# Weight-block sums by accumulating transfers in a seven-product feed-forward kernel

## The chip, the cores and the metric

The kernel runs on one core of one Trainium2 chip. A core has a matrix engine (TensorE; PE in the profile, its weight loads PEld), VectorE (DVE), ScalarE (ACT), GpSimd (POOL) and SyncE (SP), which here only issues transfers. Sixteen DMA engines move data between DRAM and the on-chip memory (SBUF); transfers can be issued from the queues of SP, ACT and POOL. The metric is the device time of one execution in microseconds (us); lower is better.

## The reference

One step of a two-layer decoder trunk over 544 tokens (512 of a prompt, 32 of samples), model width 1024. Each layer is a half feed-forward, a mixer and another half feed-forward, so there are four feed-forward phases, all of this form:

```python
def swiglu(x, w_gu, w_down):
    gate, up = jnp.split(x @ w_gu, 2, axis=-1)
    return (jax.nn.silu(gate) * up) @ w_down

def macaron_half(h, g, w_gu, w_down):
    return h + 0.5 * swiglu(rms_norm(h, g), w_gu, w_down)
```

`w_gu` is 1024 x 5632 (2816 gate columns, then 2816 up columns), `w_down` 2816 x 1024, all in float32. The mixer of the first layer is a gated MLP beside a state-space scan; that of the second is pooling beside windowed attention, whose scores get a bias from a small table by distance. In the kernel that bias is a skewed view of a pattern of 16 heads x 383 values, written 128 times in a row to DRAM.

## The kernel before, in words

**Products.** Every operand is split into a rounded part `h` and a remainder `l`; a product is three matmuls per 128 rows of the contraction (h·h, h·l, l·h). The splits of weights are `wparts` (ACT makes `wh` at L234, DVE makes `wl` at L235).

**Seven products for eight.** The gate and up matmul is done by a Strassen-like scheme. A block `f` is 128 gate and 128 up columns (22 blocks a phase, 88 in all). Its weights form a 2 x 2 of blocks: gate or up, by even or odd 128-row tiles of the contraction (`g0, g1, u0, u1`). The other operand is a 2 x 2 too: even or odd tiles, by the two halves of the tokens (272 each). Four of the seven left operands are sums of weight blocks, made on GpSimd (`sums7`, L224 to L227): S1 = u0 + u1, S2 = S1 - g0, S3 = g0 - u0, S4 = g1 - S2. The right operands' sums are made on DVE by `pair7` (L325 to L328). Each product runs over 4 tiles, 12 matmuls.

**Staging.** `load7` brings a block with two transfers of 512 KB on SP's queue into a stage tile `S` (two buffers); the sums lie in pool `sp` (one buffer each before). The split weights lie in pool `wu` (12 buffers each of `wh` and `wl`). The last operand of a block read from `S` is A22, so it frees the stage for the block two further on. The pools `wu`, `sd`, `sp`, `hl` and `rot` of a feed-forward group share memory with the pools of the mixer before it; the stage does not.

**Order.** `ffn` runs a list of jobs: per block seven products in the order A11, S2, S3, S1, A12, S4, A22 (A22 after the first job of the next block), and between them the down products of the parts that are ready. Loads are traced 17 jobs ahead of the matmuls (`LOADS`), splits 10 (`AHEAD`). The first block of a phase makes six products together (`p_first`). A planner turns the traced program into one fixed order per engine, by priorities and a simulated timeline; on the chip each engine follows its order and waits where data isn't there yet. Copies out of PSUM and gate functions are traced with high priority on ACT and DVE, among the splits.

**Groups.** The phases run as f10, even mixer, f20 and f11 (one group, so f11's loads run ahead of the border), odd mixer, f21.

**Side work.** During f10, from job 12 on, `ffn` advances a generator `mid` by one step per job. It loads four rows of parameters from ACT's queue (L408), later transposes them, and then makes the bias pattern (`bias_pattern`): small loads on POOL, one matmul, one add (L1161), and one transfer of 3064 KB from 16 partitions of SBUF to DRAM on POOL's queue (L1163). At the beginning GpSimd also adds up the squares for the norm (L307, L309).

Of the kernel before, what the change touches and what calls it, by code (L numbers as in the profile page):

```python
# [92 lines left out]
class Trunk:  # L93
    MIX = lambda r, a, u, l: (("wp", "wp", 2), ("rot", "rot", r), ("aux", "aux", a), ("uu", "uu", u), ("ld", "ld", l),
                              ("sm", "sm", 1))
    POOLS = {"even": MIX(4, 18, 3, 5), "odd": MIX(6, 14, 4, 5)}
    POOLS["f"] = (("wu", "wu", 12), ("sd", "sd", 2), ("sp", "sp", 1), ("hl", "hl", 7), ("rot", "rot", 7))

    RIGHT = {"A11": "B11", "S2": "T2", "S3": "T3", "S1": "T1", "A12": "B21", "S4": "B22", "A22": "N4"}
    PARTS = ((0, 3), (3, 6), (6, 9), (9, 12), (12, 15), (15, 18), (18, 22))  # L100
# [110 lines left out]
    def load7(self, w, f):  # L211

        s = self.stg.tile([P, 8, 256], F32, name=self.nm("S"), tag="S")
        for q in range(2):
            c0 = q * DFF + f * P
            self.nc.sync.dma_start(s[:, :, q * P:(q + 1) * P], w[:, c0:c0 + P].rearrange("(k p) m -> p k m", p=P))
        return s

    def sums7(self, s):

        G = self.nc.gpsimd
        g0, g1, u0, u1 = s[:, 0::2, 0:P], s[:, 1::2, 0:P], s[:, 0::2, P:], s[:, 1::2, P:]
        t = {n: self.sp.tile([P, 4, P], F32, name=self.nm(n), tag=n) for n in ("S1", "S2", "S3", "S4")}
        G.tensor_tensor(t["S1"], u0, u1, op=ALU.add)  # L224
        G.tensor_tensor(t["S2"], t["S1"], g0, op=ALU.subtract)  # L225
        G.tensor_tensor(t["S3"], g0, u0, op=ALU.subtract)  # L226
        G.tensor_tensor(t["S4"], g1, t["S2"], op=ALU.subtract)  # L227
        return {"A11": g0, "A12": g1, "A22": u1, **t}

# [52 lines left out]

    def gain(self, n, k):
        c = self.col[("ffn1_norm", "mix_norm", "ffn2_norm")[n % 3]]
        return c[:, n // 3 * 8 + k:n // 3 * 8 + k + 1]
# [28 lines left out]
    def pair7(self, j, n):  # L314

        nc = self.nc
        S, V, G = nc.scalar, nc.vector, nc.gpsimd
        x0, x1 = self.x[2 * j], self.x[2 * j + 1]
        g0, g1 = self.gain(n, 2 * j), self.gain(n, 2 * j + 1)
        A, B, D, E = (self.tmp(s) for s in ("fa", "fb", "fd", "fe"))  # L320
        lo_, hi_ = slice(0, HT), slice(HT, T)
        S.activation(A[:, lo_], x0[:, lo_], AF.Copy, scale=g0)
        S.activation(E[:, lo_], x0[:, hi_], AF.Copy, scale=g0)  # L323
        S.activation(B, x1, AF.Copy, scale=g1)
        V.tensor_tensor(A[:, hi_], E[:, lo_], A[:, lo_], op=ALU.subtract)  # L325
        V.tensor_tensor(D[:, lo_], B[:, hi_], A[:, hi_], op=ALU.subtract)
        V.tensor_tensor(D[:, hi_], B[:, hi_], E[:, lo_], op=ALU.subtract)
# [5 lines left out]
        for src, names in ((A, ("B11", "T1")), (B, ("B21", "B22")), (D, ("T2", "T3"))):  # L333
# [105 lines left out]
    def pair_jobs(self, gu, f, first, ph):  # L439
# [72 lines left out]
        def p_first():  # L512
# [89 lines left out]
    def ffn(self, steps, mid=None):  # L602
# [4 lines left out]
        for i, (_, _, run) in enumerate(jobs):  # L607
# [540 lines left out]
    def bias_pattern(self):  # L1148
# [13 lines left out]
        scr = self.dr.tile([16, P * 383], F32, name="scr")  # L1162
        nc.gpsimd.dma_start(scr.rearrange("h (r e) -> h r e", e=383), self.bc(pat[:16, :383], 1, P))  # L1163
        self.skew = scr[:, 127:127 + P * 382].rearrange("h (r e) -> h r e", e=382)
# [490 lines left out]
```

## Time and profile before

| | before |
|---|---|
| median of 3 runs | 2374.7 us (2369.0 to 2376.09) |
| the profiled execution | 2374.62 us, its span 2372.8 us |
| mean granted TensorE clock | 0.972 |
| busy: PE, DVE, ACT, POOL | 2267.3, 1802.6, 1099.4, 683.8 us |
| moved by DMA | 224.23 MB, mean 94 GB/s |
| GpSimd adds of weight blocks (L224 to L227) | 352, between 118.4 and 142.5 us per line |
| the bias pattern's transfer | 3064 KB, 33.5 us from issue to landing |

The span runs from the first to the last instruction of the profiled execution. In the rows of the profile a group is a line of the kernel with its engine, operation, written and read tiles, the count after an x, busy time, mean duration in ns, and after the bar the idle time before it with what ended it. A queue (SPq, POOLq) is an engine's issuing side. The share of DMA is the mean busy share of the 16 engines.

### The profile page before, as it was taken

The numbers are of one execution on the slowest core, as the hardware profiler recorded it, in microseconds if no ns is written. First come the engines' busy times: TensorE is split into PE (matmuls) and PEld (weight loads), VectorE is DVE, ScalarE is ACT, GpSimd is POOL, SyncE is SP. The second block draws the span as 40 slices with busy tenths as digits, with TensorE's granted clock in tenths as the row PEclk, the third lists the DMA queues.
The fourth block names the chain that finished last, engine by engine and source line by source line (L and its number), as shares of the span: only waits on it lengthen the run. The fifth ranks groups of instructions, "written<-read, shape, count | busy, mean of one in ns | idle before, by whom it ended". The sixth has DMA issues, their size and how long they took to land.

```text
span 2372.8 us, 43129 instructions
## 1 busy us (share of the span) xinstructions
PE 2267.3 (96%) x17292; PEld 2183.8 (92%) x17292; DVE 1802.6 (76%) x2993; ACT 1099.4 (46%) x2106; POOL 683.8 (29%) x551
## 2 busy tenths in 40 slices
PE   4969999999999989999998999999999998999998
PEld 3969999998779989999998999999988988999998
DVE  8958887766457769888879988886478657988884
ACT  4524444444336454444446444444255555444442
POOL 5323331004331015333323333322033004333331
PEclk6989999999999999999999999999999988999999
DMA  3453323321432222332331323234313213232321
GB/s 106 97 110 101 105 82 102 123 75 55 124 115 91 93 85 88 102 105 88 98 110 54 105 88 98 87 101 135 121 54 102 92 58 101 82 105 87 105 83 65
DMA packets 309241, 224.23 MB, mean 94 GB/s; under 512 B 11256, under 2 KB 301392, under 8 KB 309040
## 3 DMA queue, kind: packets, MB, share of 16 engines
q1 hardware_dynamic: 302856, 203.85, 28.2%
q0 software_dynamic: 5936, 17.55, 3.0%
q8 instruction: 135, 2.21, 0.4%
q14 instruction: 66, 0.54, 0.1%
q10 hardware_dynamic: 248, 0.07, 0.0%
HBM read 203.69 MB, written 17.75 MB: 93 GB/s over the span
## 4 chain that ended last, share of the span: by engine, by line
PE 79%; DVE 8%; issue 7%; DMA 3%; ACT 1%; POOL 1%; SPq 0%; POOLq 0%; DVEq 0%; ACTq 0%
PE acc L206 39%; PE ps L244 33%; DVE wl L235 2%; DMA S<-in_ffn_w_gu_dram 2%; DVE l L254 1%; PE ps L1118 1%; PE ps L1350 1%; PE ps L1394 1%; PE ps L827 1%; PE ps L1389 1%; PE ps L819 0%; PE ps L348 0%; ACT wh L234 0%; DVE wl L192 0%; PE acc L244 0%
## 5 line engine op out<-in xcount | busy, mean ns | idle before, releaser
L244 PE MATMUL ps<-h,wh 128*128 128x272 f32 x2384 | 690.0, 291 | 35.2 <-ACT u L480 19.3
L244 PE MATMUL ps<-l,wh 128*128 128x272 f32 x2384 | 690.0, 290 | 0.0
L244 PE MATMUL ps<-h,wl 128*128 128x272 f32 x2384 | 685.1, 290 | 0.0
L206 PE MATMUL acc<-h,wh 128*128 128x272 f32 x2832 | 600.6, 293 | 9.0 <-ACT wh L191 3.4
L206 PE MATMUL acc<-l,wh 128*128 128x272 f32 x2832 | 601.7, 292 | 0.5 <-DVE l L254 0.5
L234 ACT ACTIVATE wh<-S 128x512 fp32r<-128x512 f32 x616 | 381.3, 629 | 469.6 <-PE ps L244 270.3
L206 PE MATMUL acc<-h,wl 128*128 128x272 f32 x2832 | 596.6, 291 | 0.4 <-DVE wl L192 0.4
L235 DVE TENSOR_TENSOR wl<-S,wh 128x512 fp32r<-128x512 f32 x616 | 534.3, 877 | 67.9 <-ACT wh L234 65.7
L244 PEld LDWEIGHTS ps<-h,wh 128*128 128x128 f32 x2384 | 452.8, 190 | 40.2 <-ACT u L480 19.9
L206 PEld LDWEIGHTS acc<-h,wh 128*128 128x128 f32 x2832 | 448.2, 190 | 21.9 <-issue 11.2
L206 PEld LDWEIGHTS acc<-l,wh 128*128 128x128 f32 x2832 | 449.9, 190 | 11.3 <-issue 9.6
L206 PEld LDWEIGHTS acc<-h,wl 128*128 128x128 f32 x2832 | 448.6, 189 | 6.7 <-issue 5.3
L244 PEld LDWEIGHTS ps<-l,wh 128*128 128x128 f32 x2384 | 453.6, 190 | 0.3
L244 PEld LDWEIGHTS ps<-h,wl 128*128 128x128 f32 x2384 | 451.9, 190 | 0.0
L226 POOL TENSOR_TENSOR S<-S 128x512 f32<-128x512 f32 x88 | 135.6, 1541 | 654.1 <-DMA S<-in_ffn_w_gu_dram 434.5
L557 DVE SCALAR_TENSOR_TENSOR x<-acc,x 128x544 f32<-128x544 f32 x224 | 160.4, 717 | 105.9 <-PE acc L206 105.5
L235 DVE TENSOR_TENSOR wl<-D,wh 128x384 fp32r<-128x384 f32 (+1 forms) x224 | 188.8, 846 | 39.3 <-ACT wh L234 30.5
L224 POOL TENSOR_TENSOR S<-S 128x512 f32<-128x512 f32 x88 | 142.5, 1619 | 254.1 <-ACT fe L323 118.2
L234 ACT ACTIVATE wh<-D 128x384 fp32r<-128x384 f32 (+1 forms) x224 | 119.6, 537 | 169.8 <-PE ps L244 128.8
L191 ACT ACTIVATE wh<-S 128x1024 fp32r<-128x1024 f32 x89 | 93.3, 1050 | 197.9 <-PE acc L206 156.4
L227 POOL TENSOR_TENSOR S<-S,S 128x512 f32<-128x512 f32 x88 | 118.4, 1345 | 121.4 <-DVE wl L235 120.3
L225 POOL TENSOR_TENSOR S<-S,S 128x512 f32<-128x512 f32 x88 | 126.9, 1442 | 6.6 <-DVE wl L235 0.7
(466 smaller groups left out, 2413.9 us busy)
## 6 DMA issues: line engine op xcount, KB each, us to landing
S<-in_ffn_w_gu_dram SPq DMA_DIRECT2D x176, 512.0 KB
D<-in_ffn_w_down_dram SPq DMA_DIRECT2D x96, 384.0 KB
S<-in_ev_w_in_dram SPq DMA_DIRECT2D x18, 1024.0 KB
S<-in_od_w_in_dram SPq DMA_DIRECT2D x10, 1024.0 KB
D<-in_ffn_w_down_dram SPq DMA_DIRECT2D x16, 512.0 KB
S<-in_ev_w_out_dram SPq DMA_DIRECT2D x8, 1024.0 KB
S<-in_od_w_out_dram SPq DMA_DIRECT2D x8, 1024.0 KB
xd<-x POOLq DMA_DIRECT2D x16, 272.0 KB, 2.5
```

The source lines that it names most:

```text
L191: nc.scalar.activation(hi[:, :nk, :n], src, AF.Copy)
L206: self.nc.tensor.matmul(acc[a][:, :HT] if type(acc) is list else acc[:, a, :HT], w[:, k, :], r[:, a * HT:(a + 1) * HT], start=k == order[0 ...
L224: G.tensor_tensor(t["S1"], u0, u1, op=ALU.add)
L225: G.tensor_tensor(t["S2"], t["S1"], g0, op=ALU.subtract)
L226: G.tensor_tensor(t["S3"], g0, u0, op=ALU.subtract)
L227: G.tensor_tensor(t["S4"], g1, t["S2"], op=ALU.subtract)
L234: self.nc.scalar.activation(hi, src, AF.Copy)
L235: self.nc.vector.tensor_tensor(lo, src, hi.bitcast(F32), op=ALU.subtract)
L244: self.nc.tensor.matmul(acc, a[:, j, :], r, start=start and j == 0 and q == 0, stop=stop and j == 3 and q == 2, skip_group_check=True)
L254: nc.vector.tensor_tensor(l, src, h.bitcast(F32), op=ALU.subtract)
L557: nc.vector.scalar_tensor_tensor(two(self.x[m]), acc[:, :, :HT], 0.5, two(self.x[m]), op0=ALU.mult, op1=ALU.add)
L827: PE.matmul(psy[:, hh * 64:hh * 64 + 64], es[hh // 4][:, (hh % 4) * P:(hh % 4 + 1) * P], xd[:, hh * 64:hh * 64 + 64], start=True, stop=True)
```

## The change

It has three parts.

1. `sums7` is gone. `load7` now issues six loads on SP's queue (512 KB of gate rows into the stage, 256 KB each into S1, S2, S3, S4 with one of their terms, 256 KB of u1) and then four accumulating transfers on POOL's queue: S1 += u1 and S3 += g0 from DRAM, S2 += S1 and S4 += S2 inside SBUF. S1 lies in the half of the stage that u0 used to fill. `sp` holds three tiles with two buffers each for four with one; `wu` has 11 buffers for 12.
2. An accumulate only adds, so the signs move: `pair7` scales with negated gains (two more columns made once), its differences become sums and negated sums, and the gate rows come out negative, which `Silu` undoes with `scale=-1.0`.
3. The bias pattern goes out in 16 transfers of 8 rows each, one per step of the generator. `ffn` queues what a step issues on POOL behind the latest S4 accumulate (`self.late`) traced so far; the parameter rows are loaded from POOL's queue for ACT's.

```diff
-    POOLS["f"] = (("wu", "wu", 12), ("sd", "sd", 2), ("sp", "sp", 1), ("hl", "hl", 7), ("rot", "rot", 7))
+    POOLS["f"] = (("wu", "wu", 11), ("sd", "sd", 2), ("sp", "sp", 2), ("hl", "hl", 7), ("rot", "rot", 7))
...
-        for q in range(2):
-            c0 = q * DFF + f * P
-            self.nc.sync.dma_start(s[:, :, q * P:(q + 1) * P], w[:, c0:c0 + P].rearrange("(k p) m -> p k m", p=P))
-        return s
-
-    def sums7(self, s):
-
-        G = self.nc.gpsimd
-        g0, g1, u0, u1 = s[:, 0::2, 0:P], s[:, 1::2, 0:P], s[:, 0::2, P:], s[:, 1::2, P:]
-        t = {n: self.sp.tile([P, 4, P], F32, name=self.nm(n), tag=n) for n in ("S1", "S2", "S3", "S4")}
-        G.tensor_tensor(t["S1"], u0, u1, op=ALU.add)
-        G.tensor_tensor(t["S2"], t["S1"], g0, op=ALU.subtract)
-        G.tensor_tensor(t["S3"], g0, u0, op=ALU.subtract)
-        G.tensor_tensor(t["S4"], g1, t["S2"], op=ALU.subtract)
-        return {"A11": g0, "A12": g1, "A22": u1, **t}
+        v = w.rearrange("(j q p) m -> q p j m", q=2, p=P)
+        g, u = slice(f * P, (f + 1) * P), slice(DFF + f * P, DFF + (f + 1) * P)
+        t = {n: self.sp.tile([P, 4, P], F32, name=self.nm(n), tag=n) for n in ("S2", "S3", "S4")}
+        t["S1"] = s[:, 4:8, P:]
+        nc.sync.dma_start(s[:, :, 0:P], w[:, g].rearrange("(k p) m -> p k m", p=P))
+        for n, q, c in (("S1", 0, u), ("S2", 0, g), ("S3", 0, u), ("S4", 1, g)):
+            nc.sync.dma_start(t[n], v[q, :, :, c])
+        nc.sync.dma_start(s[:, 0:4, P:], v[1, :, :, u])
+        nc.gpsimd.dma_start(t["S1"], v[1, :, :, u], accum_op=ALU.add)
+        nc.gpsimd.dma_start(t["S3"], v[0, :, :, g], accum_op=ALU.add)
+        nc.gpsimd.dma_start(t["S2"], t["S1"], accum_op=ALU.add)
+        self.late = nc.gpsimd.dma_start(t["S4"], t["S2"], accum_op=ALU.add)
+        return {"A11": s[:, 0::2, 0:P], "A12": s[:, 1::2, 0:P], "A22": s[:, 0:4, P:], **t}
...
-        V.tensor_tensor(A[:, hi_], E[:, lo_], A[:, lo_], op=ALU.subtract)
-        V.tensor_tensor(D[:, lo_], B[:, hi_], A[:, hi_], op=ALU.subtract)
-        V.tensor_tensor(D[:, hi_], B[:, hi_], E[:, lo_], op=ALU.subtract)
-        V.tensor_tensor(E[:, hi_], B[:, lo_], D[:, lo_], op=ALU.subtract)
+        V.tensor_tensor(A[:, hi_], E[:, lo_], A[:, lo_], op=ALU.add)
+        V.scalar_tensor_tensor(D[:, lo_], B[:, hi_], -1.0, A[:, hi_], op0=ALU.mult, op1=ALU.subtract)
+        V.tensor_tensor(D[:, hi_], E[:, lo_], B[:, hi_], op=ALU.add)
+        V.scalar_tensor_tensor(E[:, hi_], B[:, lo_], -1.0, D[:, lo_], op0=ALU.mult, op1=ALU.subtract)
...
-                S.activation(st["g"], st["g"], AF.Silu)
+                S.activation(st["g"], st["g"], AF.Silu, scale=-1.0)
...
-                next(mid, None)
+                with self.tc.issue_after(self.late.ins):
+                    next(mid, None)
...
-        nc.gpsimd.dma_start(scr.rearrange("h (r e) -> h r e", e=383), self.bc(pat[:16, :383], 1, P))
+        s3 = scr.rearrange("h (r e) -> h r e", e=383)
+        for r in range(0, P, 8):
+            nc.gpsimd.dma_start(s3[:, r:r + 8], self.bc(pat[:16, :383], 1, 8))
+            yield
...
-        yield from self.columns_gen(("b_norm_g", "c_scale", "a_ln_g", "a_ln_b"), self.TT)
+        yield from self.columns_gen(("b_norm_g", "c_scale", "a_ln_g", "a_ln_b"), self.TT, self.nc.gpsimd)
```

More of the change, by code (lines that the diff above doesn't have):

```diff
@@ L96 @@
     POOLS = {"even": MIX(4, 18, 3, 5), "odd": MIX(6, 14, 4, 5)}
-    POOLS["f"] = (("wu", "wu", 12), ("sd", "sd", 2), ("sp", "sp", 1), ("hl", "hl", 7), ("rot", "rot", 7))
-    RIGHT = {"A11": "B11", "S2": "T2", "S3": "T3", "S1": "T1", "A12": "B21", "S4": "B22", "A22": "N4"}
+    POOLS["f"] = (("wu", "wu", 11), ("sd", "sd", 2), ("sp", "sp", 2), ("hl", "hl", 7), ("rot", "rot", 7))
+    RIGHT = {"A11": "N11", "S2": "T2", "S3": "N3", "S1": "T1", "A12": "N21", "S4": "N22", "A22": "N4"}
     PARTS = ((0, 3), (3, 6), (6, 9), (9, 12), (12, 15), (15, 18), (18, 22))
@@ L281, in rsqrt_small, with gain @@
             self.newton(out if i == 2 else r, r, ms, t)
-    def gain(self, n, k):
-        c = self.col[("ffn1_norm", "mix_norm", "ffn2_norm")[n % 3]]
+    def gain(self, n, k, sign=""):
+        c = self.col[sign + ("ffn1_norm", "mix_norm", "ffn2_norm")[n % 3]]
         return c[:, n // 3 * 8 + k:n // 3 * 8 + k + 1]
@@ L318, in pair7 @@
         x0, x1 = self.x[2 * j], self.x[2 * j + 1]
-        g0, g1 = self.gain(n, 2 * j), self.gain(n, 2 * j + 1)
+        g0, n0, n1 = self.gain(n, 2 * j), self.gain(n, 2 * j, "-"), self.gain(n, 2 * j + 1, "-")
         A, B, D, E = (self.tmp(s) for s in ("fa", "fb", "fd", "fe"))
         lo_, hi_ = slice(0, HT), slice(HT, T)
-        S.activation(A[:, lo_], x0[:, lo_], AF.Copy, scale=g0)
+        S.activation(A[:, lo_], x0[:, lo_], AF.Copy, scale=n0)
         S.activation(E[:, lo_], x0[:, hi_], AF.Copy, scale=g0)
[L324 to L327, printed above, removed]
-        V.tensor_tensor(E[:, hi_], B[:, lo_], D[:, lo_], op=ALU.subtract)
+        S.activation(B, x1, AF.Copy, scale=n1)
+        V.tensor_tensor(A[:, hi_], E[:, lo_], A[:, lo_], op=ALU.add)
+        V.scalar_tensor_tensor(D[:, lo_], B[:, hi_], -1.0, A[:, hi_], op0=ALU.mult, op1=ALU.subtract)
+        V.tensor_tensor(D[:, hi_], E[:, lo_], B[:, hi_], op=ALU.add)
+        V.scalar_tensor_tensor(E[:, hi_], B[:, lo_], -1.0, D[:, lo_], op0=ALU.mult, op1=ALU.subtract)
         if j % 2 == 0:
@@ L332, in pair7 @@
         ops = {}
-        for src, names in ((A, ("B11", "T1")), (B, ("B21", "B22")), (D, ("T2", "T3"))):
+        for src, names in ((A, ("N11", "T1")), (B, ("N21", "N22")), (D, ("T2", "N3"))):
             h, l = self.split(src)
@@ L397, in columns, with columns_gen @@
             pass
-    def columns_gen(self, names, alloc):
+    def columns_gen(self, names, alloc, eng=None):
         nc, I = self.nc, self.I
@@ L407, in columns_gen @@
             n = src.shape[0] * src.shape[1] // P
-            nc.scalar.dma_start(rows[r:r + n, :P], src.rearrange("a (m p) -> (a m) p", p=P))
+            (eng or nc.scalar).dma_start(rows[r:r + n, :P], src.rearrange("a (m p) -> (a m) p", p=P))
             off[nme] = (r, n)
@@ L418, in columns_gen @@
             self.col[k] = cols[:, o:o + n]
+            if k in ("ffn1_norm", "ffn2_norm"):
+                self.col["-" + k] = self.const.tile([P, n], F32, name=self.nm("ncol"))
+                nc.vector.tensor_scalar(self.col["-" + k], cols[:, o:o + n], -1.0, None, op0=ALU.mult)
     def store_x(self, m):
@@ L448, in load @@
         def load():
-            st["s"] = self.load7(gu, f)
+            st["t"] = self.load7(gu, f)
         def parts(n):
             def go():
-                if "t" not in st:
-                    st["t"] = self.sums7(st["s"])
                 st[n] = self.wparts(st["t"][n])
```

3 lines of the change are left out of this document (2 added, 1 removed).

## The prediction

> **What bounds the kernel now.** I read the page's totals first, then busy time in stretches of 50 us, then the chain of waits and the idle time inside the stretches that are not full. On the page:
>
> ```profile
> span 2372.8 us, 43129 instructions
> PE 2267.3 (96%) x17292; PEld 2183.8 (92%) x17292; DVE 1802.6 (76%) x2993; ACT 1099.4 (46%) x2106; POOL 683.8 (29%) x551
> PE 79%; DVE 8%; issue 7%; DMA 3%; ACT 1%; POOL 1%; SPq 0%; POOLq 0%; DVEq 0%; ACTq 0%
> ```
>
> TensorE is idle for 2372.8 - 2267.3 = 105.5 us in all; a change that removes no matmul can win that, plus the matmuls run at a lowered clock. Busy time in stretches (stretch and length, then per engine busy us and instructions in the order PE, PEld, DVE, ACT, POOL; then granted clock, DMA share, GB/s) shows where it lies:
>
> ```profile
> 50.00:100.00 50.00, 44.21 (x312) 41.93 (x312) 47.23 (x65) 26.77 (x50) 22.27 (x17) 0.92 0.25 74
> 100.00:150.00 50.00, 31.46 (x236) 30.46 (x236) 23.25 (x39) 12.94 (x26) 9.58 (x8) 0.84 0.77 129
> 200.00:250.00 50.00, 50.00 (x402) 50.00 (x401) 39.85 (x62) 23.20 (x45) 17.67 (x14) 1.00 0.32 96
> 850.00:900.00 50.00, 42.50 (x318) 41.39 (x317) 39.61 (x57) 26.20 (x47) 12.73 (x8) 0.93 0.27 80
> 900.00:950.00 50.00, 45.83 (x339) 45.01 (x338) 45.54 (x67) 24.33 (x49) 24.78 (x16) 0.93 0.30 88
> 1250.00:1300.00 50.00, 41.97 (x278) 39.42 (x277) 46.89 (x80) 31.68 (x59) 12.10 (x8) 0.90 0.22 64
> 1950.00:2000.00 50.00, 43.60 (x314) 42.35 (x313) 34.71 (x54) 25.47 (x44) 17.85 (x11) 0.93 0.27 79
> 2000.00:2050.00 50.00, 44.79 (x331) 43.81 (x330) 47.84 (x69) 26.18 (x51) 19.69 (x14) 0.93 0.31 90
> ```
>
> The third row is the feed-forward (FFN) steady state: TensorE full, clock 1.00, 402 matmuls in 50 us, POOL at 17.67. There neither a faster VectorE nor a free GpSimd moves the end. The others are short of 402, and (402 - n) x 50/402 gives their price: 20.6 us at 100 to 150, 11.2 at 50 to 100, 18.3 at 850 to 950, 15.4 at 1250 to 1300, 19.8 at 1950 to 2050. The gains have to come from there.
>
> **The hole at 100 to 150.** The chain, the GpSimd issue and its landing, and fine stretches:
>
> ```profile
> 107.25 33.95 DMA S<-in_ffn_w_gu_dram
> 106.45 1.04 POOL L1163 DMA_DIRECT2D scr<-pat  x1 [2.40 <-DVE pat L1161]
> scr<-pat POOLq DMA_DIRECT2D x1, 3064.0 KB, 33.5
> 126.00:128.00 2.00, 2.00 (x18) 2.00 (x17) 0.00 (x0) 0.00 (x0) 0.00 (x0) 1.00 1.00 112
> 128.00:130.00 2.00, 0.68 (x6) 0.46 (x4) 0.00 (x0) 0.00 (x0) 0.00 (x0) 1.00 0.97 110
> 140.00:142.00 2.00, 0.00 (x0) 0.00 (x0) 0.00 (x0) 0.00 (x0) 0.63 (x1) 0.50 1.12 359
> PE ps L244 <- ACT u L480: 18.5, 1, 18.5
> ```
>
> The bias pattern holds all DMA engines (share 1.00, but 112 GB/s) for 33.5 us; a weight load issued a moment later lands only behind it, at 359 GB/s. TensorE lives on prepared operands until 128.7, 22 us after the issue, then idles 18.5 us and restarts at clock 0.50. Its line names ACT, which itself sits behind a late sum in its queue.
>
> **The change, part by part.** *Bias pattern in 16 parts.* Engine time stays 33.5 us, 2.1 us a part. Each part is queued on POOL behind the latest S4 accumulate traced so far, one part per job, and a block has 7 + 56/22 = 9.5 jobs. So some 9 parts, 19 us, may leave back to back after one block's S4 and the rest a block later. 19 us is less than the 22 us TensorE lasted, so most of the hole closes; accumulates behind a burst in the same queue are late, which keeps part of it. Ends: 0 (parts still make one hog) and 20.6; I take **14**, as both bursts (19 and 15 us) lie nearer the covered 22 us than the 33.5. In a sentence apart: the Trainium skill ("DMA: Bandwidth & Descriptors", Queues, rings and completion order) says an engine alternates between queues only at packet boundaries, a packet holding up to 64 descriptors; by that, small parts let the weight loads in between and the gain would be nearer 20.6 than 14, and the trace agrees so far as the load got no share while the big transfer lasted.
>
> *The GpSimd adds leave.* 88 x 4 of them, gone from beside VectorE:
>
> ```profile
> 18.88 1.56 DVE L325 TENSOR_TENSOR fa<-fe,fa 128x272 f32<-128x272 f32 x1
> 44.85 0.43 DVE L325 TENSOR_TENSOR fa<-fe,fa 128x272 f32<-128x272 f32 x1
> L225 POOL TENSOR_TENSOR S<-S,S 128x512 f32<-128x512 f32 x3 | 4.5, 1509 | 0.1
> 1247.05 1.45 DVE fa L325
> 1248.50 1.45 DVE fd L327
> 1266.47 1.44 DVE fd L326
> 1267.91 1.71 DVE l L254
> ```
>
> One VectorE add takes 1.56 us while a GpSimd add of 1.5 us runs and 0.43 us otherwise: some 1.1 us each. From 14 to 57 us each of the four lines ran 3 times (the third row is one of them), 12 adds, up to 13 us of a VectorE that is busy throughout; the 7 GpSimd adds of the sum of squares stay. From 50 to 100 TensorE lost 11.2 us with VectorE at 47.23 of 50. The ends are 0 (ScalarE or the new chain takes over) and 24; I take **12**, half, since two engines feed TensorE there. At 1250 the four pieces of the chain shown carry about 1.1 us too much each, 4.4 us, and the operands were prefetched across the phase border, so no new chain stands in the way: **5** (0 to 15.4).
>
> *The new chain.* Per block SP issues 6 loads (512 + 5 x 256 KB) for 2 (1024 KB); GpSimd issues 4 accumulates of 256 KB, S2 after S1, S4 after S2. Nothing in the trace accumulates. The nearest rows, the load now, and the steady beat:
>
> ```profile
> L428 POOL DMA_DIRECT2D out_y_prompt_dram<-ot x8 | 6.1, 768 | 57.6 <-DVE ot L427 52.1 <-issue 5.4
> out_y_prompt_dram<-ot POOLq DMA_DIRECT2D x8, 256.0 KB, 2.6
> kc<-in_cache_k_win_dram POOLq DMA_DIRECT2D x4, 256.0 KB, 5.3
> 160.10 1.19 SPq L216 DMA_DIRECT2D S<-in_ffn_w_gu_dram  x2
> 166.39 1.28 POOL L226 TENSOR_TENSOR S<-S 128x512 f32<-128x512 f32 x1 [9.32 <-DMA S<-in_ffn_w_gu_dram]
> 175.64 0.99 SPq L216 DMA_DIRECT2D S<-in_ffn_w_gu_dram  x2
> 160.10:256.61 96.51, 96.51 (x772) 96.36 (x771) 81.06 (x122) 45.89 (x90) 34.92 (x24) 1.00 0.33 99
> ```
>
> The last row holds 24 GpSimd adds, 6 blocks: 16.1 us a block. 1 MB needs 6.3 us from issue to use, of which bytes about 3.5 (300 GB/s at share 1), so 2.8 fixed. S1's operand, 768 KB deep in the queue, lands after 5.4 us. With 2.6 to 5.3 us for an accumulate S2 is ready 10.6 to 16 us after the first load; I take 4 each, the middle of store and load: 13.4, and S4 at 17.4. The load of a block waits for the last operand (A22) of the block two before it; 175.64 is that moment one block on, when S2 of the block loaded at 160.10 is next in ScalarE's queue: 15.5 us, and about 17.7 before two blocks of 32.2 us stretch. So it is hidden, by the second buffer of the stage and of the sums, at a margin of 4 us. S4, four jobs on, has more. GpSimd's own time, 4 x 0.77 us and its waits, delays only what queues there: the next accumulates and the bias parts. SP's 6 issues of about 0.5 us fit into 16.1.
>
> Engine time per block: now 0.33 x 16.1 = 5.3 us for 1.59 MB; with 0.79 MB more 8.0; four accumulates as copies 3.5 more: 11.5 of 16.1, hidden. The other end, at the pattern's 91 GB/s (3064 KB in 33.5 us), would be 11.5 for them, 19.5 together. I take the copies: same rows of 512 B as the store of 2.6 us. Apart from that: the Trainium skill ("Collectives: The Full Stack", Part 3, why ReduceScatter is half of AllGather) holds that an add inside a transfer costs a second source read and halves the rate; by that the accumulates take 7.0, together 15.0 of 16.1, still hidden but with nothing to spare, and no run here shows it yet.
>
> *Starts at 875 and 1974.* Here no prefetch covers the chain:
>
> ```profile
> 875.48 1.52 POOL L224 TENSOR_TENSOR S<-S 128x512 f32<-128x512 f32 x1 [118.24 <-ACT fe L323]
> 881.96 1.59 POOL L227 TENSOR_TENSOR S<-S,S 128x512 f32<-128x512 f32 x1
> 889.68 2.55 PE ps L244 x14
> 1974.42 1.55 POOL L224 TENSOR_TENSOR S<-S 128x512 f32<-128x512 f32 x1 [42.07 <-PE acc L206]
> 1978.52 1.27 POOL L227 TENSOR_TENSOR S<-S,S 128x512 f32<-128x512 f32 x1
> 1985.00:1990.00 5.00, 4.92 (x22) 4.61 (x22) 3.50 (x6) 1.67 (x4) 4.46 (x2) 0.50 0.15 36
> ```
>
> The adds waited for the memory of the phase before, and were done at 883.5 and 1979.8. Now the loads into that memory wait: free at 875.5, operands at 879, S2 at 883, S4 at 887, split by 888 to 889, where the first products began at 889.7. At 1974 the same steps end at 1988, where they began about 1985: 3 us late. The next blocks arrive 2 to 4 us later than now, and VectorE gains its 1.1 us per removed add. Net, from -7 to +10 at each: **+3** and **0**.
>
> *The rest.* One weight buffer fewer (11) shortens the lookahead by one product, 1.5 us, hidden in steady state. Negative gate columns: two tiny VectorE operations at the beginning, 0.3 us. Four row loads go from ACT's queue to POOL's; nothing waits.
>
> **Sum**, against the profiled execution of 2374.6 us (1.8 outside the span; the median shown is 2374.7): 2374.6 - 14 - 12 - 5 - 3 - 0 + 0.3 = **2341**.
>
> **Rivals.** *B, the chain is too long (slower).* If an accumulate takes more than (17.7 - 5.4)/2 = 6.2 us, ScalarE reaches S2's split before its data, the copies out of PSUM queue behind it and TensorE stops in every block. Each us beyond stretches two blocks by 2 us, so 1 us a block, over some 76 steady blocks: 7 us an accumulate gives +65, 2406; 8 gives +140, 2480. It outweighs the gains from 6.6 us. For: two rows reach 5.3, and an accumulate also reads its target. Against: the store of the same rows takes 2.6, and the margin. *C, the DMA engines saturate (slower).* At 91 GB/s 3.4 us a block too much, x 80 = 272, about 2610; at 130 GB/s it just fits. *D, the starts eat it.* Late first sums cost 7 each at 875 and 1974 and the pattern's parts, competing with 11.5 busy us in 16.1, keep their hole: 2374.6 - 17 + 14 = 2371.6. *E, the change does not do what it says:* the planner leaves the parts in one row, the hole stays at about 20: 2355.
>
> **How the numbers follow.** Forecast 0.50, E 0.10, D 0.10, B 0.22, C 0.08. The time is the forecast's, 2341; its own range is 2310 to 2365, the low end with the first start whole (24), the hole whole (20.6) and most of what 875 and 1974 can add. The whole range reaches up to 2440 (accumulates of 7.4 us) and leaves out C and B's tail, 0.15, and a little below. No change is within 0.3%, 7 us: faster 0.60 (forecast, E), same 0.10 (D), slower 0.30 (B, C).
>
> **What would show it.** Right: steady stretches at 402 matmuls, clock 1.00, DMA share near 0.7; no stretch under 350 between 100 and 150; VectorE's adds near 0.43 everywhere; SP's first load to the last accumulate's landing under 20 us. Wrong: ScalarE's splits waiting for accumulates in every block, fewer than 402 matmuls per 50 us with a DMA share near 1, or TensorE idle again while bias parts land.

## The result, and the profile after

The changed kernel takes **2491.2 us** (2480.1 to 2507.1), the kernel before 2375.4 in the same comparison: ratio 1.0498, 95% interval 1.0437 to 1.0559. The forecast was 2341, its range 2310 to 2440; the change is slower, and by more than the range held.

The page of the changed kernel: its totals, and the first two DMA queues (packets, MB, share of 16 engines).

```profile
span 2478.3 us, 44140 instructions
PE 2287.1 (92%) x17292; PEld 2201.2 (89%) x17292; DVE 1608.3 (65%) x2995; ACT 1087.8 (44%) x2106; POOL 590.0 (24%) x570
DMA packets 602496, 385.82 MB, mean 156 GB/s; under 512 B 22824, under 2 KB 583296, under 8 KB 602288
q1 hardware_dynamic: 443656, 273.08, 37.9%
q0 software_dynamic: 158448, 109.87, 31.0%
```

VectorE did lose its burden: 1608 us busy for 1803. TensorE idles 191 us for 105. The second queue, GpSimd's, takes 31.0% of all engines, 768 us. Before it carried 17.55 MB at 3.0% of 2372.8, 71 us; by their packets' times the 352 accumulates so hold all 16 engines for 697 / 352 = **1.98 us** each, or 132 GB/s for 256 KB. Busy time in stretches, of the changed kernel and, in the last two lines, of the kernel before:

```profile
50.00:100.00 50.00, 35.92 (x262) 35.12 (x261) 26.11 (x48) 18.76 (x34) 15.47 (x13) 0.90 0.94 193
100.00:150.00 50.00, 40.85 (x278) 39.29 (x279) 27.68 (x50) 18.50 (x36) 19.05 (x26) 0.86 0.93 175
150.00:200.00 50.00, 31.67 (x221) 31.38 (x220) 20.51 (x37) 12.98 (x26) 13.20 (x15) 0.76 0.92 151
200.00:250.00 50.00, 50.00 (x402) 50.00 (x401) 35.06 (x63) 22.83 (x44) 13.93 (x12) 1.00 0.94 201
900.00:950.00 50.00, 36.96 (x258) 35.60 (x257) 29.48 (x53) 20.82 (x37) 12.10 (x11) 0.86 0.88 192
1400.00:1450.00 50.00, 44.56 (x341) 44.16 (x340) 32.49 (x58) 21.20 (x42) 13.81 (x12) 0.97 0.93 192
...
150.00:200.00 50.00, 50.00 (x397) 49.85 (x396) 44.72 (x66) 23.82 (x47) 19.43 (x14) 0.99 0.32 96
1400.00:1450.00 50.00, 50.00 (x401) 50.00 (x401) 41.23 (x62) 23.49 (x45) 18.51 (x14) 1.00 0.32 96
```

The stretch from 200 is full, so the kernel can run at its old pace. The starts are worse than before (262 matmuls for 312 from 50), the hole at 100 to 150 (236 matmuls before, 397 in the stretch behind it) is now 278 and 221, and stretches that were steady before, such as 1400 to 1450, lose 60 matmuls, 7.5 us. Of the first 46 stretches of 50 us, 20 held 400 matmuls or more before, and 9 do now. What they wait for, in the waits of ScalarE and of SP's queue (us in all, times, longest), and in the accumulates' landings (count, KB, median us from issue to landing):

```profile
ACT wh L235 <- DMA S<-S: 326.1, 83, 23.0
SPq L223 <- DMA S<-S: 529.7, 75, 15.8
```

```profile
S<-in_ffn_w_gu_dram POOLq DMA_DIRECT2D x176, 256.0 KB, 5.8
S<-S POOLq DMA_DIRECT2D x176, 256.0 KB, 5.7
```

ScalarE's splits stop for an accumulate inside SBUF (`S<-S`) in 83 places, 62 of them (282 us) for S2 and 21 (44 us) for S4, with 88 blocks in all. One such stall, in the lists of instructions of SP, GpSimd and ScalarE (start, duration, engine, line, operation; in brackets what it waited for):

```profile
1404.94 0.92 SPq L223 DMA_DIRECT2D S<-in_ffn_w_gu_dram  x2
1425.06 4.40 SPq L223 DMA_DIRECT2D S<-in_ffn_w_gu_dram  x3
...
1401.93 1.29 POOL L225 DMA_DIRECT2D S<-in_ffn_w_gu_dram  x1 [1.49 <-DVE u L511]
1410.09 1.29 POOL L226 DMA_DIRECT2D S<-in_ffn_w_gu_dram  x1 [6.87 <-DMA S<-in_ffn_w_gu_dram]
1410.84 1.86 POOL L227 DMA_DIRECT2D S<-S  x1
1421.63 0.87 POOL L228 DMA_DIRECT2D S<-S  x1 [8.93 <-DMA S<-S]
...
1421.45 1.15 ACT L235 ACTIVATE wh<-S 128x512 fp32r<-128x512 f32 x2 [9.64 <-DMA S<-S]
```

S1 (L225) is issued at 1401.9. S2 (L227) stands in the queue behind S3 (L226) of the next block, which waits 6.9 us for a load that SP sent out only around 1404.9; S2 goes at 1410.8 and ends at 1421.4, 10.6 us later, when ScalarE's split starts after 9.6 us of waiting. From S1's issue to S2's use: 19.5 us. SP's next three loads of this kind leave only at 1425.1; over the whole run such loads (L223) wait 529.7 us for accumulates, with all that SP has behind them.

### The profile page after: what moved, and what is told of

Same layout as the page of the kernel before. It is cut to its first block, busy times and chain, and to the rows that moved or that the text cites. A ratio compares the mean times of both kernels' runs of the same rounds, so it can differ in the third digit from the quotient of the medians.

```text
span 2478.3 us, 44140 instructions
## 1 busy us (share of the span) xinstructions
PE 2287.1 (92%) x17292; PEld 2201.2 (89%) x17292; DVE 1608.3 (65%) x2995; ACT 1087.8 (44%) x2106; POOL 590.0 (24%) x570
## 3 DMA queue, kind: packets, MB, share of 16 engines
q0 software_dynamic: 158448, 109.87, 31.0%
## 5 line engine op out<-in xcount | busy, mean ns | idle before, releaser
L245 PE MATMUL ps<-h,wh 128*128 128x272 f32 x2384 | 701.2, 297 | 94.5 <-ACT u L482 59.1
L245 PE MATMUL ps<-l,wh 128*128 128x272 f32 x2384 | 700.8, 294 | 0.0
L245 PE MATMUL ps<-h,wl 128*128 128x272 f32 x2384 | 699.7, 294 | 0.3 <-DVE wl L236 0.3
L236 DVE TENSOR_TENSOR wl<-S,wh 128x512 fp32r<-128x512 f32 x616 | 417.2, 688 | 334.3 <-ACT wh L235 294.7
L245 PEld LDWEIGHTS ps<-h,wh 128*128 128x128 f32 x2384 | 462.5, 195 | 102.2 <-ACT u L482 64.6
L245 PEld LDWEIGHTS ps<-l,wh 128*128 128x128 f32 x2384 | 464.8, 195 | 0.3
L245 PEld LDWEIGHTS ps<-h,wl 128*128 128x128 f32 x2384 | 464.0, 195 | 0.5 <-DVE wl L236 0.5
L225 POOL DMA_DIRECT2D S<-in_ffn_w_gu_dram x88 | 119.0, 1352 | 492.8 <-DMA S<-in_ffn_w_gu_dram 204.2
L227 POOL DMA_DIRECT2D S<-S x88 | 117.6, 1336 | 302.8 <-DMA S<-in_ffn_w_gu_dram 180.8
L226 POOL DMA_DIRECT2D S<-in_ffn_w_gu_dram x88 | 125.1, 1422 | 155.3 <-DMA S<-in_ffn_w_gu_dram 69.2
L236 DVE TENSOR_TENSOR wl<-D,wh 128x384 fp32r<-128x384 f32 (+1 forms) x224 | 127.3, 569 | 51.0 <-PE acc L207 33.5
L228 POOL DMA_DIRECT2D S<-S x88 | 76.9, 877 | 293.8 <-DMA S<-S 260.2
```

What stands on the lines that cost most here:

```text
L225: nc.gpsimd.dma_start(t["S1"], v[1, :, :, u], accum_op=ALU.add)
L226: nc.gpsimd.dma_start(t["S3"], v[0, :, :, g], accum_op=ALU.add)
L227: nc.gpsimd.dma_start(t["S2"], t["S1"], accum_op=ALU.add)
L228: self.late = nc.gpsimd.dma_start(t["S4"], t["S2"], accum_op=ALU.add)
L236: self.nc.vector.tensor_tensor(lo, src, hi.bitcast(F32), op=ALU.subtract)
L245: self.nc.tensor.matmul(acc, a[:, j, :], r, start=start and j == 0 and q == 0, stop=stop and j == 3 and q == 2, skip_group_check=True)
```

## The experiments

The kernel before took about 2375 us in all comparisons.

**One: take the load of the accumulates away, keep their chain.** A quarter of the rows, or plain copies in place of the adds.

```diff
-        nc.gpsimd.dma_start(t["S1"], v[1, :, :, u], accum_op=ALU.add)
+        nc.gpsimd.dma_start(t["S1"][:, 0:1], v[1, :, 0:1, u], accum_op=ALU.add)   # a_quarter, and so for all four
+        nc.gpsimd.dma_start(t["S1"], v[1, :, :, u])                               # a_copy, and so for all four
```

> The changed kernel, but each of the four accumulates moves only one of its four row tiles (64 KB for 256 KB), so three quarters of the sums are left out and the output is wrong; queues, waits and order of the chain stay. Theory T (the DMA engines are full: 8.0 us of plain loads and, from the queue's share in the profile after, 4 x 2.0 us of accumulates in a block of 16.1): the need falls to about 10 us a block, the share from 0.95 to about 0.65, and the time to 2340 to 2380. Theory R (the chain of dependent transfers and the waits of SP and ScalarE on it are the limit, as in rival B): the fixed part of each step stays, some 3 us of 5.7, the splits still wait in every block, 2420 to 2470.

> The changed kernel with the four accumulates as plain copies of the same 256 KB on the same queue with the same waits (the sums are left out, each copy overwrites). T: a copy takes half the engine time of an accumulate, 3.5 us for four against 7.9, need 11.5 of 16.1 us, share about 0.72, time 2345 to 2400, SP's waits on the last step mostly gone. R: same number of steps, each landing after 3 to 5 us: above 2420.

Measured: 2363.5 (ratio 0.9963, 0.9948 to 0.9979) and 2369.0 (0.9972, 0.996 to 0.9984). The queue and the landings of the copies:

```profile
q0 software_dynamic: 34544, 109.87, 15.2%
```

```profile
S<-in_ffn_w_gu_dram POOLq DMA_DIRECT2D x176, 256.0 KB, 3.9
S<-S POOLq DMA_DIRECT2D x176, 256.0 KB, 3.2
```

The same 109.87 MB take 15.2% of 2369.1 us, 360 us, so a copy takes (360 - 71) / 352 = 0.82 us of the engines where an accumulate takes 1.98, and lands after 3.2 to 3.9 us and not 5.7. It also leaves in 34544 packets and not 158448. With the light transfers the chain loses no time in steady stretches, as this one of `a_copy` shows:

```profile
1400.00:1450.00 50.00, 50.00 (x401) 50.00 (x400) 35.07 (x63) 22.97 (x44) 8.39 (x12) 1.00 0.70 208
```

T as expected, R (2420 to 2470, and above 2420) fell. But neither kernel comes near 2341, and the later runs correct what T says of the cause.

**Two: the bias pattern alone.** The sixteen parts behind the S4 add in the kernel before; one transfer in the changed kernel.

```diff
+                with self.tc.issue_after(self.late.ins):      # b_split, late = the S4 add
+                    next(mid, None)
...
-        for r in range(0, P, 8):                              # a_one
-            nc.gpsimd.dma_start(s3[:, r:r + 8], self.bc(pat[:16, :383], 1, 8))
+        nc.gpsimd.dma_start(scr.rearrange("h (r e) -> h r e", e=383), self.bc(pat[:16, :383], 1, P))
```

> The kernel before with the bias pattern alone in 16 parts, each queued on GpSimd behind the latest S4 add. If small parts let weight loads in between, the hole of 20.6 us at 100 to 150 closes by 14 or more: 2355 to 2362. If the parts still hold the engines as one (33.5 us in bursts of 19 and 15), it stays: 2370 to 2378.

> The changed kernel with the bias pattern in one transfer again. T: with engines at a share of 0.95 the pattern's 33.5 us are paid by TensorE in either form, so within 12 us of the changed kernel (2480 to 2503). R: engines have room between the steps of the chain, so the parts are what keeps the hole small, and one transfer costs about 20 more: 2505 to 2515.

Measured: 2362.8 (0.9945, 0.9924 to 0.9967), and 2493.3 against the changed kernel's 2491.2. The stretch in the kernel before with the parts:

```profile
100.00:150.00 50.00, 44.57 (x334) 43.34 (x333) 33.77 (x55) 18.90 (x38) 21.07 (x26) 0.96 0.84 159
```

334 matmuls for 236, 12.2 us, which is about the whole gain (10.9 us by the medians of its comparison, 13 by its ratio). In the changed kernel the same split shows no gain within the spread of the runs (2480 to 2507): in either form a hole stays between 100 and 200.

**Three: the pattern from 128 partitions**, as an alternative to the parts, and with it the sums half by transfer.

```diff
-        nc.tensor.matmul(ps[:16, :383], tab, t5[0][:32, :383], start=True, stop=True)
+        nc.tensor.matmul(ps[:, :383], tab8, t5[0][:32, :383], start=True, stop=True)      # b_wide, tab8 = each column of tab eight times
...
+        nc.gpsimd.dma_start(scr.rearrange("h (i r e) -> (h i) r e", i=8, e=383), self.bc(pat[:, :383], 1, 16))
...
-        nc.gpsimd.dma_start(t["S2"], t["S1"], accum_op=ALU.add)                          # a_half: S2, S4 on GpSimd
+        nc.gpsimd.tensor_tensor(t["S2"], t["S1"], s[:, 0::2, 0:P], op=ALU.add)
...
```

> The kernel before; the bias pattern is computed on 128 partitions (each of its 16 rows eight times) and written to DRAM in one transfer from all of them, 16 copies from each, in place of 128 copies from each of 16 partitions. W (the 33.5 us came from reading 16 partitions only): the transfer takes 10 to 14 us, the hole between 100 and 150 closes from 236 matmuls to 320 or more, 2353 to 2363 us, as with the sixteen parts. V (the 33.5 us are those of rows of 1.5 KB written to DRAM, whatever the source): 30 us or more, 2370 to 2378.

> The changed kernel with S1 and S3 by accumulating transfers and S2 and S4 by GpSimd again (their two loads are dropped). A block needs about 5.3 + 0.8 + 2 x 1.98 = 10.1 of 16.1 us of the DMA engines. T (full engines were the cause): 2355 to 2372 us, DMA share 0.6 to 0.66 in steady stretches, the bias parts and the next group's loads find room. R (a chain through accumulates costs by itself): two of its four steps are left, 2400 to 2440.

> S1 and S3 by accumulating transfers, S2 and S4 on GpSimd (2358), and the bias pattern in one transfer from 128 partitions in place of the sixteen parts. If the parts still cost something between 100 and 200 (342 and 319 matmuls there, against 362 and 402 with the wide transfer in the kernel before), 100 us hold 100 matmuls more and the time is 2344 to 2352; if the starts take that back, 2355 to 2360.

Measured: 2361.3 (0.9949, 0.9931 to 0.9966), 2358.2 (0.9937, 0.9916 to 0.9957) and **2349.4** (0.9888, 0.9867 to 0.9909). The last one, with both, is the fastest kernel here that leaves nothing of the computation out. The pattern lands after 18.9 us in the first (33.5 before): later than W's 10 to 14, but the hole holds 362 matmuls. With only S1 and S3 accumulated, no accumulate waits for another, and the engines have less to move (DMA share 0.64 in a steady stretch); R for `a_half` (2400 to 2440) fell, but this run changes both things at once.

**Four: what the GpSimd adds cost.** The sums left out of the kernel before; then made, but read by nobody.

```diff
-        return {"A11": g0, "A12": g1, "A22": u1, **t}
+        return {"A11": g0, "A12": g1, "A22": u1, "S1": u0, "S2": g0, "S3": u0, "S4": g1}   # b_idle; b_nosums without the adds
```

> The kernel before without the four GpSimd adds of each block: S1 to S4 are simply the blocks u0, g0, u0 and g1, so the output leaves the sums out; nothing else changes (the bias pattern in one transfer). The most that taking the adds off GpSimd can give, with no accumulate in their place. F (the prediction's term: VectorE slowed by GpSimd's adds holds TensorE at the starts): -12 at the first start, -5 at 1250, and some 6 at each of the starts at 875 and 1974 where the first sums no longer stand in the chain: 2345 to 2358. N (VectorE is faster but TensorE waits there for something else): 2368 to 2378, with VectorE's busy time lower between 50 and 100 and at 850 to 950 and TensorE's counts as before (312; 318 and 339).

> The kernel before with its four GpSimd adds per block still made, but read by nobody: the products take u0, g0, u0 and g1 in their place, so the output leaves the sums out. It stands between the kernel before (2374) and the one without the adds (2333). V (the prediction's term: VectorE, slowed by GpSimd's adds running beside it, holds TensorE at the starts): the adds still run beside it, so 2362 to 2376. L (the starts wait for the sums themselves, one add after another behind the load): nobody waits any more, so 2330 to 2342 although VectorE stays slow.

Measured: 2332.7 (0.9827, 0.98 to 0.9854) without the adds, faster than even F had it (2345 to 2358), and 2375.9 (1.0009, 0.9996 to 1.0022) with adds that nobody reads. The two splits of VectorE, without the adds and with the unread ones:

```profile
L231 DVE TENSOR_TENSOR wl<-S,wh 128x512 fp32r<-128x512 f32 x616 | 419.7, 688 | 79.1 <-ACT wh L230 76.4
```

```profile
L235 DVE TENSOR_TENSOR wl<-S,wh 128x512 fp32r<-128x512 f32 x616 | 551.0, 906 | 34.0 <-ACT wh L234 32.3
```

Two starts without the adds, where the kernel before had 312 and 278 matmuls:

```profile
50.00:100.00 50.00, 50.00 (x392) 49.03 (x391) 39.84 (x75) 28.22 (x53) 1.04 (x1) 0.99 0.43 114
1250.00:1300.00 50.00, 49.06 (x392) 48.84 (x391) 40.20 (x76) 27.26 (x51) 0.00 (x0) 1.00 0.36 109
```

That speaks for V and against L: nobody waits for the sums in either kernel, and the 43 us go with the adds' running beside VectorE, 906 ns for 688 per split. Unread adds could also hold the stage longer, but in the waits of SP's queue in `b_idle` no load waits for GpSimd. `b_nosums` also does without the pool `sp`, and what that is worth was not tried alone.

**Five: the changed kernel without accumulates,** then with accumulates of both sizes into spare DRAM buffers that nobody reads.

```diff
-        nc.gpsimd.dma_start(t["S1"], v[1, :, :, u], accum_op=ALU.add)    # a_noacc: all four left out
...
+        self.late = nc.gpsimd.dma_start(z[0], t["S1"], accum_op=op)      # a_unread4, z = four of 16 spare DRAM buffers; a_unread1 a quarter of each
+        with self.tc.issue_after(self.late.ins):
+            for i, c in ((1, g), (2, u), (3, g)):
+                self.late = nc.gpsimd.dma_start(z[i], v[i % 2, :, :, c], accum_op=op)
```

> The changed kernel without its four accumulates; the loads of S1 to S4 and the bias parts stay, and the products take the loaded blocks, so the output leaves the sums out. A block needs about 8.0 of 16.1 us of the DMA engines. L (with the quarter-size accumulates it was the chain of transfers at the group starts that took back what VectorE won): 2315 to 2340, the stretches 50 to 100 and 900 to 950 near 390 matmuls. O (something else of the change holds the starts: more loads, one weight buffer fewer, the bias parts): 2350 to 2368, as with the quarter-size accumulates (2363.5).

> The changed kernel; its four accumulates per block are issued by GpSimd as before, at a quarter of the size, but into spare DRAM buffers that nobody reads; the products take the loaded blocks, so the output leaves the sums out. It lies between the kernel without accumulates (2324) and the one whose products wait for quarter-size accumulates (2363.5). W (at the starts ScalarE waits for one landing after another, and that is the 39 us): nobody waits here, 2322 to 2334. I (GpSimd's issues or the engine time of the small accumulates): 2350 to 2366.

> The same at full size: four accumulates of 256 KB per block that nobody reads, and the products take the loaded blocks, so the output leaves the sums out. The engines need about 8.0 + 4 x 2.06 = 16.2 of 16.1 us a block. E (full engines delay the loads whatever waits for the sums; the kernel before lost 91 to such traffic): 2324 + 91, 2400 to 2440, DMA share 0.95 or more. Z (most of the loss is the wait for the accumulates' landings): 2335 to 2380 at the same share. The rest to 2491 would be the landings' own part.

Measured: 2324.1 (0.9784, 0.9766 to 0.9802), 2314.3 (0.9752, 0.9724 to 0.978), 2351.1 (0.9902, 0.9873 to 0.9932). So L, W and Z, with 2314.3 below W's range (2322 to 2334): small transfers cost nothing while nobody waits for them, and full-size ones cost 27 us, not the 91 that E took over from the paced traffic below. A steady stretch of `a_unread4`:

```profile
200.00:250.00 50.00, 50.00 (x402) 50.00 (x401) 35.15 (x62) 22.96 (x44) 14.36 (x12) 1.00 1.11 213
```

TensorE is full at a DMA share of 1.11, above that of the changed kernel in any row shown. Busy engines alone are not the cause. That `a_unread1` is 10 us below `a_noacc` fits its count between 100 and 150 (402 matmuls for 293): its bias parts stand behind accumulates, those of `a_noacc` behind loads. It wasn't tested by itself.

**Six: added traffic in the kernel before.** Two tries to fill the engines without touching the sums.

```diff
...
+        for i in range(4):                                                       # b_traffic, issued with the load, beside three copies on SP's queue
+            self.nc.gpsimd.dma_start(self.yy[(n + i + 5) % 12], v[i % 2, :, :, ...], accum_op=ALU.add)
...
+        with self.tc.issue_after(s4.ins):                                        # b_paced, behind the S4 add and two copies
...
+            for i in range(4):
+                G.dma_start(self.yy[8 + (4 * n + i) % 16], self.v[i % 2, :, :, c], accum_op=ALU.add)
```

> The kernel before, its sums on GpSimd as they were; added beside each weight block, for nothing that the output uses: three copies and four accumulating transfers of 256 KB each, from the weights in DRAM into spare buffers in DRAM. No sum and no product waits for them. By the costs measured so far a block then needs about 5.3 + 3 x 0.82 + 4 x 1.98 = 15.7 of its 16.1 us of the 16 DMA engines, as in the changed kernel. T (full DMA engines alone cost the time, through whatever else needs a transfer at the starts of the groups): 2430 to 2490 us, DMA share 0.9 or more in the steady stretches. R (the time was lost because the sums wait for a chain of transfers, and not because the engines are full): 2375 to 2395, with 402 matmuls in steady stretches at the same DMA share. If an accumulate into DRAM costs less than one into on-chip memory, the share will say so, and the run then tells less.

> The kernel before, its sums on GpSimd as they were; behind the S4 add of each block GpSimd's queue also issues two copies and four accumulates of 256 KB from the weights into spare DRAM buffers that nobody reads. By the costs of the run with the unpaced traffic (2.06 us an accumulate, 1.25 us a copy from DRAM to DRAM) a block needs 5.3 + 2.5 + 8.2 = 16.0 of 16.1 us of the DMA engines, as in the changed kernel (15.9), now spread over the whole run. T (full engines alone are enough): 2420 to 2520 us, DMA share near 1 in the feed-forward stretches, the loss at the starts of the groups. R (full engines cost only what waits for the accumulates): 2375 to 2400.

Measured: 2758.7 (1.1628, 1.1605 to 1.1651) and 2466.2 (1.0378, 1.0355 to 1.0401). Neither tells what it was made for. Unpaced, all the transfers ran in the first 1100 us at shares up to 1.3. The paced run fell into T's range, but ScalarE waited there for GpSimd's adds:

```profile
ACT wh L247 <- POOL S L226: 125.9, 35, 7.4
```

The transfers' issues stand between the adds on GpSimd's queue (POOL busy 1222 us for 684), so the sums came late. `a_unread4`, where no add of weight blocks is on that queue, corrects the reading.

**Seven: more buffers,** so that SP's loads need not wait for the accumulate that still reads their buffer.

```diff
-    ("wu", "wu", 11), ("sd", "sd", 2), ("sp", "sp", 2)
+    ("wu", "wu", 9), ("sd", "sd", 2), ("sp", "sp", 3)     # a_sx3; a_s2x3: 10, and a third buffer for S2 alone
```

> The changed kernel with a third buffer for S2 and one weight buffer fewer (10). The load of a block's S2 then no longer waits for the last accumulate of the block two before, in a queue in which the next stage loads stand behind it (529.7 us of such waits in the changed kernel). Q (late landings and queues that wait for them are the loss): the wait falls under 200 us and the time to 2400 to 2460. F (full DMA engines are the loss): 2475 to 2505 at a DMA share of 0.9 to 1.0.

> The changed kernel with three buffers for each of S2, S3 and S4 and two weight buffers fewer (9). Q: one block more of lookahead for the whole chain, 2380 to 2440, with ScalarE's waits for accumulates well under the 326 us of the changed kernel; the DMA share then passes 1 in steady stretches, as with the unread accumulates. F: 2475 to 2505, or more for the two buffers taken away.

Measured: 2508.0 (1.0565, 1.0543 to 1.0587) and 2500.4 (1.054, 1.0505 to 1.0574). Q fell: SP's wait for accumulates goes from 529.7 to 381.0 and 404.5 us only, ScalarE's from 326 to 259 and 282, and the time rises. Both times lie at F's (full engines, 2475 to 2505) or just above, but the next runs take F away. Whether the third buffers gave something that the weight buffers taken away cost again was not tried.

**Eight: cut the links.** S2 and S4 accumulate from DRAM in place of S1 and S2; all transfers and readers stay.

```diff
-        nc.gpsimd.dma_start(t["S2"], t["S1"], accum_op=ALU.add)
-        self.late = nc.gpsimd.dma_start(t["S4"], t["S2"], accum_op=ALU.add)
+        nc.gpsimd.dma_start(t["S2"], v[1, :, :, u], accum_op=ALU.add)                   # a_flat; a_qflat a quarter
+        self.late = nc.gpsimd.dma_start(t["S4"], v[0, :, :, g], accum_op=ALU.add)
```

> The changed kernel at full size, but S2 and S4 accumulate from the weights in DRAM and no longer from S1 and S2, so no accumulate waits for another (the output leaves these dependences out). Same bytes, same number of accumulates, all of them read. D (the depth of the chain, two accumulates one behind the other ahead of S2, three ahead of S4): 2385 to 2440. E (each accumulate's own late landing under busy engines, whatever the depth): 2470 to 2495.

> The same with accumulates of a quarter of the size. Between the quarter-size chain (2363.5) and quarter-size accumulates that nobody reads (2314). D: 2325 to 2345. E (one landing behind the load is enough to hold the starts): 2352 to 2366.

Measured: **2385.2** (1.0042, 1.0027 to 1.0056) and 2337.7 (0.9841, 0.9824 to 0.9857). `a_flat` lands on the border of D's range, 106 us below the changed kernel. The stretch that lost 60 matmuls, and its landings:

```profile
1400.00:1450.00 50.00, 50.00 (x401) 50.00 (x400) 34.97 (x62) 23.28 (x45) 15.34 (x12) 1.00 1.01 206
```

```profile
S<-in_ffn_w_gu_dram POOLq DMA_DIRECT2D x352, 256.0 KB, 6.9
```

Each accumulate lands later than in the changed kernel (6.9 for 5.7 us), the engines move more, and TensorE is full; 21 of the first 46 stretches hold 400 matmuls or more. What stops the changed kernel is that one late transfer waits for another. The diff hides one thing that goes with the links. S2 no longer reads S1 out of the stage, so the planner sends it out ahead: in the median S2 is issued 13 us before S1, where in the changed kernel it is issued 5.8 us after it. So the 106 us are the price of the links as a whole, one landing behind another, the wait for the stage and the order of the queue; the runs don't separate these three.

Together, as differences of medians, good to a few us each (the kernel before alone goes from 2373.8 to 2376.8 over the comparisons), the last to some 10 (2480 to 2507):

| step | us | time |
|---|---|---|
| the kernel before | | 2375 |
| bias pattern in parts (`b_split`) | -12 | 2363 |
| adds gone, loads in (`a_noacc`) | -39 | 2324 |
| full accumulates, unread (`a_unread4`) | +27 | 2351 |
| read, without links (`a_flat`) | +34 | 2385 |
| links S1 to S2 to S4 (changed kernel) | +106 | 2491 |

At a quarter of the size the last three are -10, +23 and +26: 2314, 2338, 2363.5.

## Why the prediction was wrong, point by point

**"So it is hidden ... at a margin of 4 us": the step that failed.** The prediction let S2's data stand at 13.4 us after the load of the stage, against 17.7 allowed. In the changed kernel it stands at **20.3 us** in the median, and above 17.7 in 75 of the 88 blocks; in `a_copy`, with the same chain, at 14.0, and above 17.7 in 12 (from the issue of L221 to the landing of L227, paired in order). No single size made that. S1's accumulate goes out after 7.9 us and not 5.4 (5.9 in `a_copy`). S1 and S2 land after 5.1 and 5.6 us in the median, and S2 after 10.6 in the stall shown, where the prediction took 4 for each, the middle of a store at 2.6 and a load at 5.3. With these landings alone its sum would give 5.4 + 5.1 + 5.6 = 16.1, still inside 17.7. And the sum left out the order of the queue: it said GpSimd's waits delay "only what queues there: the next accumulates and the bias parts", but the next accumulates are the chain.

Rival **B** had the mechanism, at 0.22, and named the place rightly: ScalarE at S2's split, the copies out of PSUM behind it (TensorE's longest waits, 59 us in all, are for `ACT u` L482, such a copy). But it asked for more than 6.2 us an accumulate, which S1 and S2 stay below in the median, because it too let S1 go out at 5.4. Its line of 1 us a block per us gives 2491 at about 8.1 us, which was not measured, so the time doesn't confirm its price. And it had the stop in every block; the stretches that stay full show otherwise.

**"Engine time per block ... I take the copies": mis-sized term.** 3.5 us for four accumulates; measured 4 x 1.98 = 7.9, so 15.9 of 16.1 together. The other end, at the pattern's 91 GB/s, was too low a rate; rival C had it that "at 130 GB/s it just fits", and at 132 it did fit: `a_flat` and `a_unread4` run full stretches with these bytes. So **C** by itself did not happen. But an accumulate lands later than a copy, and later still on busy engines: S1 and S3 after 3.7 and 4.1 us as copies, 4.6 and 4.9 as accumulates at a DMA share of 0.64 (`a_half`), 5.1 and 6.8 in the changed kernel, 6.1 and 7.5 in `a_flat`. The chain of copies loses nothing in steady stretches, and unlinked accumulates don't either: there the loss needs both, long landings and a chain of them.

The rule quoted in the prediction, from the Trainium skill ("Collectives: The Full Stack", Part 3, why ReduceScatter is half of AllGather), gave 7.0 us for the four, nearer to the measured 7.9 than the copies. It puts the halving down to a second source read; the packets here (158448 for 34544) would speak for more and smaller pieces too. The packets of the traces tell the two apart in part (medians, 1300 to 1600 us). One of 512 B takes 65 ns in an accumulate, at a share of 0.64 in `a_half` as well as at 1.0 in `a_flat`, and 27 ns in a plain load on SP's queue; the copies go in packets of 4096 B at 159 ns, 20 ns per 512 B. If a plain load stands for a plain small piece, the smaller pieces are the lesser part of the factor, and the add is the greater.

**"Starts at 875 and 1974", gains of 3 and 0.** The start in the changed kernel, in the lists of SP, GpSimd and ScalarE:

```profile
911.58 3.60 SPq L223 DMA_DIRECT2D S<-in_ffn_w_gu_dram  x6
...
915.25 1.26 POOL L227 DMA_DIRECT2D S<-S  x1 [5.55 <-DMA S<-in_ffn_w_gu_dram]
924.63 0.87 POOL L228 DMA_DIRECT2D S<-S  x1 [3.87 <-DMA S<-S]
...
929.93 5.83 ACT L235 ACTIVATE wh<-S 128x512 fp32r<-128x512 f32 x11 [8.07 <-DMA S<-S]
```

From the loads into the freed memory to the split that waits for S4 18.3 us, where the prediction had about 13 (875.5 to 888 or 889): S2 alone takes 9.4 us from its issue to S4's. Even at a quarter of the size the starts pay: the stretches 50 to 100 and 900 to 950 with the quarter-size chain, and with the same transfers unread:

```profile
50.00:100.00 50.00, 43.84 (x312) 42.61 (x310) 31.82 (x61) 23.07 (x44) 16.07 (x22) 0.91 0.59 140
900.00:950.00 50.00, 45.25 (x339) 44.00 (x338) 35.23 (x67) 24.35 (x48) 14.59 (x17) 0.97 0.76 186
```

```profile
50.00:100.00 50.00, 49.82 (x387) 48.58 (x387) 39.94 (x75) 29.97 (x55) 15.89 (x25) 0.99 0.72 164
900.00:950.00 50.00, 50.00 (x401) 50.00 (x400) 36.93 (x65) 24.18 (x46) 10.28 (x12) 1.00 0.65 165
```

The first two have the very counts of the kernel before, 312 and 339: the chain takes back there what VectorE won. It is rival **D**'s mechanism, at 49 us (2363.5 - 2314.3). D had 14 for the starts and 14 for the pattern's parts; about 20 of the 49 lie between 100 and 200, where the parts go out (350 and 290 matmuls for 402 and 402).

**"The GpSimd adds leave: -12, -5."** Right in kind, and too small: -39 in the changed kernel, -41 in the kernel before. The prediction counted single adds of 1.1 us at two starts and halved the first; the counts without the adds rise at all four starts (392 for 312 from 50, 392 for 278 from 1250, 401 for 339 from 900 and for 331 from 2000). Cutting a bound to half because "two engines feed TensorE there" was a choice that no row carried. The Trainium skill ("SBUF — State Buffer", Who interferes with whom) says that a VectorE instruction with two SBUF inputs contends with a GpSimd instruction that reads SBUF; the split of weights has two, and 906 for 688 ns agrees.

**"Bias pattern in 16 parts: -14."** Right in the kernel before, about -12. It is short of the 20.6 to which the packet rule of the Trainium skill ("DMA: Bandwidth & Descriptors", Queues, rings and completion order) pointed: 334 matmuls still fall short of 402. The reading beside it, that the load got no share while the big transfer lasted, was wrong. From 112 to 136 us the trace before has 483 packets on the loads' queue for 531 of the pattern: they take turns one for one, as that rule has it. But a load's packet is 512 B in 27 ns and one of the pattern 4596 B in 700 ns, so the loads moved 244 KB for 2440. Parts of the pattern keep these packets (698 ns in `b_split`), so they don't let more loads in while they run; what remains is that the engines are free between them. Beside the chain the parts show no gain (2493.3 for 2491.2). So the sum added terms that are not independent.

**"The rest"**: nothing in the runs speaks against the 0.3 us; the weight buffer was not tried alone.

With no accumulate at all the kernel takes 2324, less than the forecast: the gains were undersized by 17 us in all, and the chain, which it held to be hidden in steady blocks and harmless at the starts, cost 167.

## What to carry to other kernels

A chain of transfers is costed by its landings, one behind the other in one queue, with the engines as busy as they will be then, and not by the bytes: here cutting two links at the same bytes, with the earlier start that this allows, gave back 106 of 167 us. If no row shows the operation, a middle between two other rows is not a price, and a margin smaller than the spread of those rows is no margin. Work moved off an engine helps as far as its replacement isn't serial: accumulating only the two sums that hang on nothing, with the pattern sent from 128 partitions, is 1.1% faster than the kernel before, at 2349.

## What was not expected of the hardware

- By the packets' times an accumulate of 256 KB holds the 16 engines 2.4 times as long as a copy of the same bytes on the same queue (1.98 for 0.82 us), in 4.6 times the packets over that queue, and the issue of S1's on GpSimd takes 1.35 us for 0.75 (the changed kernel, then `a_copy`):

```profile
L225 POOL DMA_DIRECT2D S<-in_ffn_w_gu_dram x88 | 119.0, 1352 | 492.8 <-DMA S<-in_ffn_w_gu_dram 204.2 <-DVE wl L236 151.9 <-issue 71.5
```

```profile
L225 POOL DMA_DIRECT2D S<-in_ffn_w_gu_dram x88 | 66.4, 754 | 736.7 <-DVE wl L236 354.5 <-DMA S<-in_ffn_w_gu_dram 231.9 <-DVE l L255 42.9
```

- The busy share of the DMA engines is no measure of what is left: `a_unread4` runs full stretches at 1.11, the changed kernel stalls at 0.93.
- A transfer that broadcasts from 16 partitions lands after 33.5 us, one of the same 3064 KB from 128 partitions after 18.9; its packets of 4596 B take 700 ns in the first and 242 in the second.
